# Weight tiles split as whole tiles instead of as two halves, in a two-block network on one core

## The chip, the cores and the metric

The kernel runs on one core of one Trainium2 chip, as one launch. The metric is device time in microseconds (us) of that launch. The profile is of one profiled execution of the same kernel.

## The reference, cut to what matters

512 tokens of width 1024 (and 256 context tokens) pass through two blocks. The first block is a mixer (a gated linear scan in both directions and a chunk-wise spatial gating), then a mixture of experts: 64 experts of width 256, of which each token uses 8, and one shared expert. The second block is a mixer of windowed attention and chunk-wise retention, then an MLP with a squared ReLU. All products are float32. The part that the change touches most:

```python
def swiglu(h, w_gu, w_down):
    gate, up = jnp.split(h @ w_gu, 2, axis=-1)
    return (jax.nn.silu(gate) * up) @ w_down

def moe_ffn(h, w_router, b_router, w_gu, w_down, w_sh_gu, w_sh_down):
    ...
    def expert_block(acc, blk):
        tok, wts, e = blk
        out = swiglu(h_pad[tok], w_gu[e], w_down[e])
        return acc.at[tok].add(out * wts[:, None].astype(out.dtype)), None
    ...
    return acc[:N] + swiglu(h, w_sh_gu, w_sh_down)
```

The other large products are of the same kind (`h @ w_in`, `y @ w_o`, `merged @ w_out`, `hdn @ w_ff2`): activations for 512 tokens against a weight matrix that is read once.

## The kernel before, in words

**A product as three.** A float32 product is made of three products of reduced values. Each operand is cut into a high part (`hi`, the value rounded by a copy) and a low part (`lo`, the value less its high part), and `mm3` (L142 to L148) issues hi x hi (L146), hi x lo (L147) and lo x hi (L148) into one accumulator. Where the weights are the second operand, as in the experts, L147 reads the low part of the weights and L148 the low part of the activations, when the names in the rows read `mm<-whi,eaT` in either order: the rows name the buffers of both operands, whichever is loaded as weights.

**A unit.** Weights come in units of 2048 values a partition, 1 MB each. `load_unit` (L113) gives a unit a raw buffer (`raw`, three of them, and two more from the pool `wraw2` in the expert layer) and issues one DMA on SP's queue. `split_unit` (L121) cuts it: `hi` is an ACT copy (L132, `whi` in the rows), `lo` a subtraction on DVE (L133, `wlo`; a few are given to POOL). A unit of 2048 values is cut in two pieces of 1024 values, each with its own `hi` and `lo` buffer, its own ACT copy and its own subtraction; the class `Rows` (L55) finds the piece in which row k of the unit lies. A unit of 1024 values (`w_branch_a`, `w_branch_b`, `w_att_up`) is one piece.

**The rings.** The buffers for pieces are the pool `wsplit`, six for `hi` and six for `lo`, taken in turn by `Turns` (L42): three units. In the expert layer `grow` (L1130) adds the pool `wsplit2` with two more, so four units. `each_unit` (L1372), which serves the four quarters of a matrix that are all in use at once, adds two of the pool `wsplit3`, taken after the first two units. A buffer is free for its next piece when the last matmul that reads it is done.

**The expert layer** (`experts`, L1170). `plan` (L1149) puts the tokens of the experts into 44 groups with 47 blocks of up to 128 rows; 64 experts have three units each, two of `w_expert_gu` and one of `w_expert_down`, 192 in all. A unit serves twelve matmuls of 512 columns for each block of its expert. For each group the program says, in this order: the first gu unit; then, by `advance`, the turning of the *previous* group's activations (`expert_turn`, L1014: two transposes `tp` on PE, then `split_ps`, L150, whose high part `eaT` is an ACT copy, L152, and whose low part `eaT` is a DVE subtraction, L153); the second gu unit; then the previous group's down unit with `eaT` as the other operand (`expert_out`, L1025), whose result is scaled by ACT into `ey`. Behind that, `expert_parts` (L1043) cuts part of the rows into `eys` (high part on ACT, L1048, low part on POOL, L1049) for a one-hot product into accumulators (`expert_add`, L1054), and the rest goes out by scattering DMAs of POOL (L1039). Tables of slots (`slot_tables`, L892 to L940: one-hots `oh` on DVE, L903, their matmuls, L908, and small sums) and gathers of rows on POOL (L981) come ahead of the groups that need them.

**Order.** Outside two stretches that are ordered by hand (ACT in the linear scan, and DVE, ACT and POOL where the two blocks meet), a planner orders each engine's instructions ahead of the run: it goes by expected durations and by the program's order as priority, and an engine then runs its instructions in that fixed order, each as its waits allow. So an instruction that is ready on the chip can stand behind one that is not, or behind a long one.

The change touches `PIECES`, `PIECE` and `Rows` (L30, L55), the pool `wsplit` in the constructor, `split_unit`, `fm_chunk` (L162, which reads the number of rows of a unit), `grow` and the line that restores the rings behind it (L1146), and `each_unit`.

Of the kernel before, what the change touches and what calls it, by code (L numbers as in the profile page):

```python
# [10 lines left out]
F = mybir.dt.float32  # L11
R = mybir.dt.float32r
# [3 lines left out]
AF = mybir.ActivationFunctionType  # L16
# [10 lines left out]
KD = D // 128  # L27
EPS = 1e-6
UNIT = 2048
PIECES = 2  # L30
PIECE = UNIT // PIECES


VEC = {}
# [7 lines left out]
class Turns:  # L42


    def __init__(self, *pools):
        self.pools = list(pools)
        self.n = 0

    def next(self):
        order = [p for p, n in self.pools for _ in range(n)]  # L50
        self.n += 1
        return order[(self.n - 1) % len(order)]


class Rows:  # L55


    def __init__(self, tiles, n, a):
        self.tiles, self.n, self.rows = tiles, n, a

    def __getitem__(self, at):
        p, k, *rest = at
        return self.tiles[k // self.n][(p, k % self.n, *rest)]


class Kernel:
    def __init__(self, ctx, tc, ins, out):
        self.tc, self.nc, self.ins, self.out = tc, tc.nc, ins, out
        self.ctx = ctx
        pool = lambda name, bufs=1, **k: ctx.enter_context(tc.tile_pool(name=name, bufs=bufs, **k))  # L70
        self.const = pool("const")
        self.raws = Turns((pool("wraw", RAW_BUFS, side="right"), RAW_BUFS))
        self.splits = Turns((pool("wsplit", SPLIT_BUFS * PIECES), SPLIT_BUFS * PIECES))
        self.dram = pool("scratch", space=DRAM)
        self.background, self.ticking = iter(()), False
        self.constants()
# [44 lines left out]
    def split_unit(self, parts, a, b, engine=None, rv=None):  # L121

        nc = self.nc
        if rv is None:
            rv = self.load_unit(parts if isinstance(parts, list) else [(None, parts)], a, b)
        n = min(a, a * PIECE // UNIT) if a * b == UNIT else a
        tiles = []
        for k in range(0, a, n):
            sp = self.splits.next()
            hi = sp.tile([128, PIECE], R, tag="hi", name="whi")[:, :n * b].rearrange("p (a b) -> p a b", a=n)  # L130
            lo = sp.tile([128, PIECE], R, tag="lo", name="wlo")[:, :n * b].rearrange("p (a b) -> p a b", a=n)
            nc.scalar.activation(hi, rv[:, k:k + n], AF.Copy)  # L132
            (engine or nc.vector).tensor_sub(lo, rv[:, k:k + n], hi.bitcast(F))  # L133
            tiles.append((hi, lo))
        hv, lv = (Rows([t[i] for t in tiles], n, a) for i in range(2))
        if not self.ticking:
            self.ticking = True
            next(self.background, None)
            self.ticking = False
        return hv, lv  # L140

    def mm3(self, ps, a, b, start, stop):  # L142

# [17 lines left out]

    def fm_chunk(self, ps, w, x, j, n=T, x0=0):  # L162

        kk = w[0].rows
        for k in range(kk):
            self.mm3(ps, [y[:, k, j * 128:(j + 1) * 128] for y in w],
                     [y[:, k, x0:x0 + n] for y in x], k == 0, k == kk - 1)
# [919 lines left out]
    def first_block(self):  # L1087

        nc, tc, ins = self.nc, self.tc, self.ins
        dram = lambda name, n, m=D: self.dram.tile([n, m], F, name=name)  # L1090
        h2d, x1d, cb = dram("h2d", T), dram("x1d", T), dram("cb", T, D - CA)
        self.g3d = dram("g3d", 1)
        rctx, hctx = ExitStack(), ExitStack()
        yT, rows = self.mixer(rctx)
        actx = ExitStack()
        pp = actx.enter_context(tc.tile_pool(name="moeps", bufs=1, space=PSUM))
        with tc.tile_pool(name="route", bufs=1) as keep:
            self.routing_state(keep)
            hp = hctx.enter_context(tc.tile_pool(name="h2T", bufs=1))

            h2T = [[hp.tile([128, KD, T // 2], R, name=f"h2T{h}{i}") for i in range(2)] for h in range(2)]
            pt = tc.tile_pool(name="b1o", bufs=1, space=PSUM)
            ap = tc.tile_pool(name="moeacc", bufs=1, space=PSUM)
            raws, splits = self.raws, self.splits
            with ExitStack() as mctx, ExitStack() as ectx:
                with pt as pt:
                    out = self.out_proj(pp, pt, yT, rows, h2T, h2d, x1d)
                    next(out)
                    rctx.close()
                    mp = mctx.enter_context(tc.tile_pool(name="moe", bufs=1, side="right"))  # L1110
                    acc, gp = [], []
                    gT = [mp.tile([128, 2, T], R, name=f"shT{i}") for i in range(2)]
                    shared = self.shared_expert(mp, pp, gp, gT, h2T)
                    for _ in range(SHARED_EARLY):
                        next(shared)
                    for _ in out:
                        pass
                gctx = ExitStack()
                gp.append(gctx.enter_context(tc.tile_pool(name="moegu", bufs=1, space=PSUM)))

                def sums():

                    gctx.close()
                    ap_ = actx.enter_context(ap)
                    acc.extend(ap_.tile([128, 512], F, name=f"acc{t}") for t in range(NT))

                rawp = ectx.enter_context(tc.tile_pool(name="wraw2", bufs=RAW2, side="right"))
                self.raws = Turns(*raws.pools, (rawp, RAW2))

                def grow():  # L1130
                    hctx.close()
                    sp = ectx.enter_context(tc.tile_pool(name="wsplit2", bufs=PIECES))
                    self.splits = Turns(*splits.pools, (sp, PIECES))
                    return ectx.enter_context(tc.tile_pool(name="moe2", bufs=1))

                def ahead():

                    more = self.raws
                    self.raws = Turns(*raws.pools)
                    self.first_raws = self.quarters("w_v_2")[:RAW_BUFS]  # L1140
                    self.first_raws = [self.load_unit([(None, w)], 4, 512) for w in self.first_raws]
                    self.raws = Turns(more.pools[1])
                    self.splits = Turns(self.splits.pools[1])

                more = self.experts(mp, pp, h2d, cb, acc, shared, gT, sums, grow, ahead, ectx)
            self.raws, self.splits = raws, splits  # L1146
        return x1d, cb, acc, more, actx.close

    def plan(self):  # L1149
# [221 lines left out]

    def each_unit(self, ctx, w, loaded=(), engines=()):  # L1372

        sp = ctx.enter_context(self.tc.tile_pool(name="wsplit3", bufs=PIECES))
        (base, n), = self.splits.pools
        loaded = [*loaded, *[None] * 4]
        engines = [*engines, *[None] * 4]
        splits = self.splits
        turns = Turns((base, n - PIECES), (sp, PIECES), (base, PIECES))
        for q, rv, e in zip(w, loaded, engines):  # L1380
            self.splits = turns
            unit = self.split_unit(q, 4, 512, e, rv)
            self.splits = splits
            yield unit
# [428 lines left out]
SPLIT_BUFS = 3  # L1813
# [146 lines left out]
```

## Time and profile before

| | |
|---|---|
| runs | 2130.84, 2125.3, 2128.33 us; median 2128.33 |
| profiled execution | 2128.15 us, span 2126.4 us, mean granted clock 0.985 |
| PE matmul, busy | 2038.1 us (96%), 10311 instructions |
| PE weight load, busy | 1663.4 us (78%) |
| DVE, busy | 1425.5 us (67%) |
| ACT, busy | 1090.8 us (51%) |
| POOL, busy | 486.2 us (23%) |
| `wlo` on DVE (L133) | 586 instructions, 728.0 us |
| `whi` on ACT (L132) | 592 instructions, 621.0 us |
| DMA | 386.68 MB, mean 182 GB/s |

The span is the time from the first to the last instruction of the profiled execution; the execution's own time holds the little that lies around it. PE is the engine of the matmuls and PEld its weight loads, which run beside them; DVE, ACT and POOL are the vector, scalar and GpSimd engines; SP issues DMAs. Matmuls overlap in their pipeline, so that PE's busy share says that it has work, not how fast that goes. An idle time is put down to the instruction whose end released the engine. L followed by a number is a line of the kernel; `split_unit` and `mm3` are helpers, so that all weights share their lines, and the names of the tiles tell products apart (`xT`, `eaT` in the expert layer; `hT`, `x`, `mg` and others elsewhere).

### The profile page before, as it was taken

The page shows a single profiled execution, that of the slowest core. Times are in us where ns is not written, and L with a number is a line of the kernel's source. Part 1 is how long each engine was busy: PE and PEld are TensorE (multiplying, and loading weights), DVE is VectorE, ACT ScalarE, POOL GpSimd, SP SyncE. Part 2 cuts the span into 40 slices and gives each one's busy share as a digit, 9 for nine tenths or more (in the row PEclk, how much of TensorE's full clock was granted, in tenths as well). Part 3 has the DMA queues.
Part 4 walks back from the last instruction along what each step waited for, and adds up shares of the span by engine and source line. Part 5 has one row for each costly group of instructions (what it writes and reads, how often), then busy time and mean ns, then how long its engine had stood idle before and what let it go on. Part 6 is the DMA issues. An engine that isn't in the chain of part 4 may idle for free. (4 is left out here: it accounts for less than half of the span.)

```text
span 2126.4 us, 28083 instructions
## 1 busy us (share of the span) xinstructions
PE 2038.1 (96%) x10311; PEld 1663.4 (78%) x10311; DVE 1425.5 (67%) x2444; ACT 1090.8 (51%) x1569; POOL 486.2 (23%) x307
## 2 busy tenths in 40 slices
PE   7999999999899999999999996999999999999998
PEld 4777888877787788877887784877788878888886
DVE  6667767647899799989999785455853345333344
ACT  7445443233387788878887884334232224232232
POOL 0322231011144343524334213011100001010110
PEclk9999999999899999999999998999999999999999
DMA  7211136633499899999999885312122333222221
GB/s 297 70 41 48 53 111 261 235 110 147 177 322 335 290 341 352 339 325 307 337 336 337 289 290 188 132 60 70 50 89 79 114 115 116 92 100 99 99 80 40
DMA packets 69713, 386.68 MB, mean 182 GB/s; under 512 B 11374, under 2 KB 12351, under 8 KB 30020
## 3 DMA queue, kind: packets, MB, share of 16 engines
q1 hardware_dynamic: 56932, 357.56, 45.6%
q0 software_dynamic: 12640, 27.29, 5.5%
q8 instruction: 82, 1.34, 0.2%
q14 instruction: 59, 0.48, 0.1%
HBM read 369.99 MB, written 23.55 MB: 185 GB/s over the span
## 5 line engine op out<-in xcount | busy, mean ns | idle before, releaser
L133 DVE TENSOR_TENSOR wlo<-raw,whi 128x1024 fp32r<-128x1024 f32 x586 | 728.0, 1258 | 252.0 <-ACT whi L132 244.0
L132 ACT ACTIVATE whi<-raw 128x1024 fp32r<-128x1024 f32 x592 | 621.0, 1057 | 385.6 <-PE mm L147 190.7
L146 PE MATMUL mm<-whi,xT 128*128 128x512 f32 (+2 forms) x536 | 219.7, 410 | 0.1
L147 PE MATMUL mm<-wlo,xT 128*128 128x512 f32 (+2 forms) x536 | 211.9, 395 | 0.0
L148 PE MATMUL mm<-whi,xT 128*128 128x512 f32 (+2 forms) x536 | 211.9, 395 | 0.0
L1039 POOL DMA_INDIRECT cb<-ey,sgi x67 | 130.9, 1954 | 233.4 <-ACT ey L1035 148.4
L146 PE MATMUL mm<-hT,whi 128*128 128x512 f32 x320 | 127.0, 397 | 0.0
L147 PE MATMUL mm<-hT,whi 128*128 128x512 f32 x320 | 125.8, 394 | 0.0
L148 PE MATMUL mm<-hT,wlo 128*128 128x512 f32 x320 | 125.5, 392 | 0.0
L147 PE MATMUL mm<-x,whi 128*128 128x512 f32 x304 | 122.5, 403 | 0.0
L148 PE MATMUL mm<-x,wlo 128*128 128x512 f32 x304 | 120.8, 398 | 0.0
L146 PE MATMUL mm<-x,whi 128*128 128x512 f32 x304 | 120.8, 397 | 0.0
L148 PEld LDWEIGHTS mm<-whi,xT 128*128 128x128 f32 (+2 forms) x536 | 96.8, 181 | 27.8
L146 PEld LDWEIGHTS mm<-whi,xT 128*128 128x128 f32 (+2 forms) x536 | 97.2, 181 | 23.1 <-DVE act L1012 0.5
L1565 POOL TENSOR_TENSOR relu<-relu 128x512 f32<-128x512 f32 x32 | 42.9, 1341 | 315.0 <-ACT relu L1563 315.0
L147 PEld LDWEIGHTS mm<-wlo,xT 128*128 128x128 f32 (+2 forms) x536 | 97.2, 181 | 22.3
L1049 POOL TENSOR_TENSOR eys<-ey,eys 128x384 fp32r<-128x384 f32 (+2 forms) x47 | 79.2, 1686 | 141.2 <-ACT eys L1048 114.3
L148 PE MATMUL mm<-whi,eaT 128*128 128x512 f32 (+2 forms) x268 | 105.8, 396 | 0.4 <-DVE eaT L153 0.2
L147 PE MATMUL mm<-wlo,eaT 128*128 128x512 f32 (+2 forms) x268 | 105.8, 395 | 0.0
L146 PE MATMUL mm<-whi,eaT 128*128 128x512 f32 (+2 forms) x268 | 105.8, 395 | 0.0
L146 PE MATMUL mm<-y,whi 128*128 128x512 f32 (+2 forms) x272 | 103.2, 380 | 0.0
L148 PE MATMUL mm<-y,wlo 128*128 128x512 f32 (+2 forms) x272 | 103.1, 379 | 0.0
(534 smaller groups left out, 4488.9 us busy)
## 6 DMA issues: line engine op xcount, KB each, us to landing
raw<-in_w_expert_gu SPq DMA_DIRECT2D x128, 1024.0 KB
raw<-in_w_expert_down SPq DMA_DIRECT2D x64, 1024.0 KB
raw<-in_w_in SPq DMA_DIRECT2D x41, 1024.0 KB
raw<-in_w_ff SPq DMA_DIRECT2D x32, 1024.0 KB
raw<-in_w_ada SPq DMA_DIRECT2D x24, 1024.0 KB
raw<-in_w_out SPq DMA_DIRECT2D x8, 1024.0 KB
raw<-in_w_v SPq DMA_DIRECT2D x4, 1024.0 KB
raw<-in_w_ret_up SPq DMA_DIRECT2D x4, 1024.0 KB
```

The lines of the kernel that those rows point to most:

```text
L132: nc.scalar.activation(hi, rv[:, k:k + n], AF.Copy)
L133: (engine or nc.vector).tensor_sub(lo, rv[:, k:k + n], hi.bitcast(F))
L146: mm(ps, ah, bh, start=start, stop=False)
L147: mm(ps, ah, bl, start=False, stop=False)
L148: mm(ps, al, bh, start=False, stop=stop)
L1039: self.nc.gpsimd.indirect_dma_start(out=cb, out_offset=bass.IndirectOffsetOnAxis(ap=gi, axis=0), in_=y[p0:p1, CA:], in_offset=None, bounds ...
L1049: last = nc.gpsimd.tensor_sub(yl, y[0:m, :CA], yh.bitcast(F))
L1565: nc.gpsimd.tensor_mul(sq, r, r)
```

## The change

A unit has one `hi` and one `lo` buffer of 2048 values instead of two of each. The rings hold as many units as before: three in `wsplit`, one more in `wsplit2` and in `wsplit3`. `self.cuts` says in how many instructions each part of a unit is written: two of 1024 values as before, into halves of the one buffer, and one of 2048 values in the expert layer, from `grow` until the rings are restored. A unit of 1024 values takes a whole buffer and is written by one instruction, as before. The order of the matmuls in the program, the raw buffers and the loads stay.

```diff
-PIECES = 2
-PIECE = UNIT // PIECES
...
-class Rows:
...
-        self.splits = Turns((pool("wsplit", SPLIT_BUFS * PIECES), SPLIT_BUFS * PIECES))
+        self.splits = Turns((pool("wsplit", SPLIT_BUFS), SPLIT_BUFS))
+        self.cuts = 2
...
-        n = min(a, a * PIECE // UNIT) if a * b == UNIT else a
-        tiles = []
+        n = a // self.cuts if a * b == UNIT else a
+        sp = self.splits.next()
+        hi, lo = (sp.tile([128, UNIT], R, tag=t, name="w" + t)[:, :a * b].rearrange("p (a b) -> p a b", a=a)
+                  for t in ("hi", "lo"))
         for k in range(0, a, n):
-            sp = self.splits.next()
-            hi = sp.tile([128, PIECE], R, tag="hi", name="whi")[:, :n * b].rearrange("p (a b) -> p a b", a=n)
-            lo = sp.tile([128, PIECE], R, tag="lo", name="wlo")[:, :n * b].rearrange("p (a b) -> p a b", a=n)
-            nc.scalar.activation(hi, rv[:, k:k + n], AF.Copy)
-            (engine or nc.vector).tensor_sub(lo, rv[:, k:k + n], hi.bitcast(F))
-            tiles.append((hi, lo))
-        hv, lv = (Rows([t[i] for t in tiles], n, a) for i in range(2))
+            nc.scalar.activation(hi[:, k:k + n], rv[:, k:k + n], AF.Copy)
+            (engine or nc.vector).tensor_sub(lo[:, k:k + n], rv[:, k:k + n], hi[:, k:k + n].bitcast(F))
...
-        return hv, lv
+        return hi, lo
...
-        kk = w[0].rows
+        kk = w[0].shape[1]
...
-                    sp = ectx.enter_context(tc.tile_pool(name="wsplit2", bufs=PIECES))
-                    self.splits = Turns(*splits.pools, (sp, PIECES))
+                    sp = ectx.enter_context(tc.tile_pool(name="wsplit2", bufs=1))
+                    self.splits = Turns(*splits.pools, (sp, 1))
+                    self.cuts = 1
...
-            self.raws, self.splits = raws, splits
+            self.raws, self.splits, self.cuts = raws, splits, 2
...
-        sp = ctx.enter_context(self.tc.tile_pool(name="wsplit3", bufs=PIECES))
+        sp = ctx.enter_context(self.tc.tile_pool(name="wsplit3", bufs=1))
...
-        turns = Turns((base, n - PIECES), (sp, PIECES), (base, PIECES))
+        turns = Turns((base, n - 1), (sp, 1), (base, 1))
```

## Rows read from the trace of the kernel before

**Rows 1.** Windows: us, busy by engine, granted clock, DMA share, GB/s.
```profile
600.00:1272.00 672.00, 668.01 (x3415) 532.01 (x3414) 605.40 (x881) 557.26 (x742) 262.91 (x148) 1.00 0.92 323
1590.00:2067.00 477.00, 475.70 (x2140) 394.10 (x2139) 182.99 (x216) 148.73 (x184) 50.59 (x38) 1.00 0.29 102
```

**Rows 2.** Waits, 600 to 1272: total us, times, longest.
```profile
ACT whi L132 <- PE mm L148: 71.2, 136, 5.5
...
PEld L908 <- DVE oh L903: 4.6, 9, 1.2
...
PEld acc L1058 <- POOL eys L1049: 2.2, 3, 1.2
...
PEld mm L148 <- DVE eaT L153: 1.9, 4, 0.7
```

**Rows 3.** Lines by form, 600 to 1272: busy us, mean ns, idle before and its releasers.
```profile
L133 DVE TENSOR_TENSOR wlo<-raw,whi 128x1024 fp32r<-128x1024 f32 x372 | 458.2, 1253 | 54.8 <-ACT whi L132 50.6
L132 ACT ACTIVATE whi<-raw 128x1024 fp32r<-128x1024 f32 x371 | 390.0, 1057 | 74.2 <-PE mm L148 71.2 <-DVE wlo L133 0.7 <-DVE srow L915 0.3
...
L1048 ACT ACTIVATE eys<-ey 128x384 fp32r<-128x384 f32 x30 | 15.7, 524 | 0.8
```

**Rows 4.** Tiles wlo and hdl: ns shortest/median/longest, first and last start.
```profile
L133 DVE TENSOR_TENSOR wlo<-raw,whi x586: 1201/1221/2776, 22.3 to 2075.7; 128x1024 fp32r<-128x1024 f32 x196
L153 DVE TENSOR_TENSOR hdl<-relu,hdh x32: 691/693/694, 1780.8 to 2078.5; 128x512 fp32r<-128x512 f32 x32
```

**Rows 5.** Timeline of ACT: start, us, instruction, [idle before, releaser].
```profile
857.66 1.06 ACT L132 ACTIVATE whi<-raw 128x1024 fp32r<-128x1024 f32 x1 [0.45 <-PE mm L148]
...
865.31 1.06 ACT L132 ACTIVATE whi<-raw 128x1024 fp32r<-128x1024 f32 x1 [0.18 <-PE mm L148]
866.28 0.37 ACT L152 ACTIVATE eaT<-tp 128x256 fp32r<-128x256 f32 x1
```

**Rows 6.** Timeline of DVE, same stretch.
```profile
858.70 4.62 DVE L133 TENSOR_TENSOR wlo<-raw,whi 128x1024 fp32r<-128x1024 f32 x4
...
866.00 2.35 DVE L133 TENSOR_TENSOR wlo<-raw,whi 128x1024 fp32r<-128x1024 f32 x2
868.27 0.42 DVE L153 TENSOR_TENSOR eaT<-tp,eaT 128x256 fp32r<-128x256 f32 x1
```

**Rows 7.** Timeline of PE and its weight loads, same stretch.
```profile
865.25 0.48 PE L146 MATMUL mm<-whi,xT 128*128 128x512 f32 x1
...
868.13 0.39 PE L146 MATMUL mm<-whi,eaT 128*128 128x512 f32 x1
868.37 0.40 PE L147 MATMUL mm<-wlo,eaT 128*128 128x512 f32 x1
...
868.74 0.19 PEld L148 LDWEIGHTS mm<-whi,eaT 128*128 128x128 f32 x1 [0.41 <-DVE eaT L153]
```

**Rows 8.** Timeline of DVE in a later group.
```profile
1016.96 0.36 DVE L153 TENSOR_TENSOR eaT<-tp,eaT 128x192 fp32r<-128x192 f32 x1
1017.24 2.35 DVE L133 TENSOR_TENSOR wlo<-raw,whi 128x1024 fp32r<-128x1024 f32 x2
```

**Rows 9.** Timeline of PE in the retention stage.
```profile
1506.44 0.60 PE L1773 MATMUL ryps<-rv,ram 128*128 128x256 f32 x2
1507.77 0.48 PE L147 MATMUL mm<-x,whi 128*128 128x512 f32 x1
```

**Rows 10.** Timeline of PE ahead of the second block's output product.
```profile
1724.03 0.50 PE L147 MATMUL mm<-wlo,mg 128*128 128x512 f32 x1 [0.54 <-DVE wlo L133]
```

**Rows 11.** Timeline of DVE and POOL in the expert layer.
```profile
855.72 2.66 DVE L133 TENSOR_TENSOR wlo<-raw,whi 128x1024 fp32r<-128x1024 f32 x1 [0.22 <-ACT whi L132]
...
856.25 1.03 POOL L1049 TENSOR_TENSOR eys<-ey,eys 96x384 fp32r<-96x384 f32 x1
```

**Rows 12.** Tile hT: ns shortest/median/longest, first and last start.
```profile
L146 PE MATMUL mm<-hT,whi x320: 387/389/501, 43.5 to 463.5; 128*128 128x512 f32 x160
...
L153 DVE TENSOR_TENSOR hT<-hm,hT x8: 671/685/693, 26.4 to 55.9; 128x512 fp32r<-128x512 f32 x8
```

More of the change, by code (lines that the diff above doesn't have):

```diff
@@ L52, in next @@
         return order[(self.n - 1) % len(order)]
-class Rows:
[L58 to L63, printed above, removed]
 class Kernel:
```

## The prediction, made before the kernel was run

> **What bounds the kernel now.** I read the windows first, because the shares of the whole span average stages with different limits. In the expert layer, here 600 to 1272 us, the reader is to see four resources near their limit at once [rows 1]: PE is busy 668.01 of 672 us, DVE 605.40 (90%), ACT 557.26 (83%), and the DMA share is 0.92. In the stretch of the MLP, 1590 to 2067 us, PE is as full (475.70 of 477) while DVE has 38% and ACT 31%. So a change that lightens DVE and ACT can matter in the expert layer alone, and there only if they hold PE up.
>
> Do they? The waits say no. ACT's own splits wait for matmuls, 71.2 us in 136 waits [rows 2]: the consumer is the slow one, and the split runs into full buffers. PE's weight loads wait little: 4.6 us for the one-hot of the tables, 2.2 for POOL's eys, 1.9 for the low part of eaT [rows 2]; no wait for whi or wlo is among PE's longest. The timeline shows the lead: the whi that starts at 857.66 [rows 5] and its wlo, done at the latest when four of them end at 858.70 + 4.62 = 863.32 [rows 6], feed the matmul at 868.13 [rows 7]. The buffers hold four units, so a unit is split up to four ahead of its use, here at least 868.13 - 863.32 = 4.8 us before it. PE bounds the expert layer; elsewhere it does so too, but for the stalls between stages.
>
> **The change, part by part.** The base is the profiled execution, 2128.15 us, of which the span is 2126.4; the median of three runs is 2128.33, so the sum serves for both.
>
> 1. Shorter work. An expert's unit of 2048 values has two ACT copies of 1.057 us and two DVE subtractions of 1.253 in the mean [rows 3], 1.221 in the median [rows 4]. No row has 2048 values, so I extend the line: ACT takes 0.524 us for 384 values and 1.057 for 1024 [rows 3], 0.83 ns a value, so about 1.057 + 0.85 = 1.91 (estimate); DVE takes 0.693 for 512 and 1.221 for 1024 [rows 4], so about 1.221 + 1.06 = 2.28 (estimate). Saved per unit: 2.11 - 1.91 = 0.20 us of ACT and 2.44 - 2.28 = 0.16 of DVE, over 64 experts x 3 units 39 and 31 us. All of it lies beside PE: 0 on the path. What it can give back is some of PE's waits for DVE, 4.6 + 1.9 [rows 2]: I take 3 us off.
>
> 2. Later release. A whole buffer is free when the last of its twelve matmuls is done, not half of it at the middle. The ring holds four units as before, so the first value of a new split comes up to half a unit later, about 1.4 us (six matmuls, 868.13 - 865.25 being one unit's twelve and 2.88 us [rows 7]). With the merged pair, wlo is complete some 1.4 + 1.91 + 2.28 - 3.6 = 2.0 us later (3.6 is about what 1.06 and two of 1.22 take now). The lead of at least 4.8 us covers it: 0. The raw buffer also returns later, and SP, which issues its loads in order, starts the next ones later by as much; ACT's waits name PE [rows 2], not a DMA, so five raw buffers cover that: 0. Without these covers it would be up to 2 us on each of 192 units.
>
> 3. What queues behind a long instruction. This is the step that costs. Between the two gu units of a group the previous group's activations are turned: PE tp, ACT eaT (high), DVE eaT (low), and three matmuls into the next unit PE needs the low part. Read one group [rows 5 to 7]: at 865.31 ACT takes a whi released by PE, so eaT starts at 866.28, right behind it; DVE takes two wlo from 866.00 (2.35 us) and eaT only at 868.27; PE's load waits 0.41 us, till 868.74. With whole units the same order reads: whi 865.31 to 867.22, eaT high to about 867.5, still ahead of its matmul at 868.13. But wlo is ready at 867.25, before eaT, and runs to 869.55; eaT low ends about 869.95, and the matmul that would start at 868.60 (one spacing after the 868.37 of [rows 7]) is 1.4 us late. Nothing can go between the halves any more. If DVE instead takes eaT first, as it does at 1016.96 before the wlo pair of 1017.24 [rows 8], it ends by 867.95 and PE loses nothing. Which comes first is set by the planner's order, and DVE in that order may still be busy until eaT is ready. Bounds over 44 groups: 0 to 44 x 1.4 = 62 us. The planner also fills PE's waits where it foresees them: in the retention stage it puts ryps matmuls between those of a gate product [rows 9]. Today only 4 loads are late for eaT [rows 2], so I take the value nearer the lower end, one group in five: 9 x 1.4 = 13 us.
>
> 4. Outside the expert layer the instructions stay; only release is coarser, and a unit of 1024 values takes a whole buffer. A product there lasts 48 matmuls, some 11 us, and three buffers leave two products of lead: 0. Where four units are wanted at once, before out_proj's tiles of the second block, PE already waits 0.54 us for a wlo at 1724.03 [rows 10]; one more wlo of 1.2 us now comes after the last release. I add 1 us, bounds 0 and 3 for the three such places.
>
> 5. GpSimd. While POOL subtracts eys for 1.03 us from 856.25, the DVE wlo of 855.72 takes 2.66 [rows 11] instead of 1.22: one of the two blocks the other. An instruction of 2.28 can hold eys up by 1.06 more. PE waits for eys 3 times now, 2.2 us [rows 2]; I take 0, bound 47 x 1.06 = 50 us of POOL time, of which PE sees at most a few.
> The Trainium skill (SBUF — State Buffer, section "SBUF: two separate sides") has a rule against the change here: DVE with two SBUF inputs and a GpSimd op share a port pair, and whichever starts first keeps it for its whole instruction while the other fully blocks. The trace agrees that they exclude each other, but in these rows DVE started first and was the one drawn out; by the rule the sum would hold up to 1.06 us more for each eys met.
>
> Sum: 2128.15 - 3 + 13 + 1 = 2139.
>
> **The rivals.**
> *Slower by waits for eaT (the forecast).* 2135 to 2190, by one to six of seven groups late; for it the order in rows 5 to 7, against it the planner's freedom.
> *No change.* Every delay stays under its lead, or PE's waits are filled: 2128 - 3 + 1 = 2126 to 2134. For it PE's 668 of 672 us; against it that eaT has no lead of four units.
> *Faster, DVE the true limit.* If DVE at 90% of the layer set the pace, its 31 us would come off: 2128 - 31 = 2097; if only half of PE's waits of some 9 us [rows 2] and a few hidden ones went, about 2120. Against it ACT waits for PE, not PE for wlo; the point from which it decides is a wlo that ends after its matmul could start. The Trainium skill (Perfetto Trace Analysis, "Identifying the Most-Contended Engine") calls matmul busy time a bad measure and would judge by weight-load busy time. That is 532 of 672, 79% [rows 1], under DVE's 90%, so by the page DVE is the most contended and 2097 the result. In the timeline matmuls follow each other at 0.24 us with no wait named [rows 7], which speaks for PE.
> *The change does not do what it says.* If one buffer made a matmul wait for both parts, the stages with two parts would start later by 1.2 us a unit wherever there is no lead, some 10 us in all. Against it: matmuls on hT begin at 43.5 us while its parts are written until 55.9 [rows 12], so a wait is for the part read.
>
> **How the numbers follow.** A measurement of this kernel can tell about 0.3% from no change, 6.4 us. Slower by waits: 0.42, and with the last rival's 0.02 the slower side has 0.44. No change 0.37. Faster 0.19, of which the full 2097 has 0.04. The prediction is the likeliest case, 2139, with its own range 2135 to 2190. For 8 in 10 I go down to 2117, which leaves out the full gain, and up to 2172, where 31 of 44 groups would be late.
>
> **What would show it.** In the expert layer's rows: 192 whi at 1.91 and 192 wlo at 2.28 us; ACT's waits on PE longer, its splits starting at unit ends; DVE and ACT busy less by some 30 and 38 us; PE loads of L148 waiting for DVE eaT, some 9 or more times at up to 1.4 us, against 4 now. PE full and those waits unchanged would make it the second case; a wait of PE for wlo would show that a lead I called safe was not; gaps in PE that DVE or POOL used to cause gone, and the time near 2120, the third. A stage outside the expert layer longer by over 3 us would make part 4 wrong.

## The result, and the profile after

The changed kernel takes 2142.33 us in the median (2141.41 to 2148.84, 4 runs) against 2127.07 before (2125.30 to 2130.84, 4 runs): the ratio is 1.0078, with a 95% interval of 1.0056 to 1.0099. It is slower, by 15 us in the medians. The profiled execution took 2141.41 us with a span of 2139.7, so 13.3 us more than the span before; the account below is made against that.

Lines have moved: `whi` is now L119 and `wlo` L120, the three products of `mm3` L131 to L133, the two parts of `eaT` L137 and L138, `oh` L888, `eys` L1034 and the one-hot product `acc` L1043. Each experiment below has its own numbers; the tile names tell.

**Where it went.** First the place. These are rows of the tile `eaT` between 590 and 1310 us, for the last product of each kernel (ns shortest/median/longest, first and last start). Before:

```profile
L148 PE MATMUL mm<-whi,eaT x268: 387/394/506, 599.6 to 1282.5; 128*128 128x512 f32 x102, 128*96 128x512 f32 x26, 128*64 128x512 f32 x6
```

After:

```profile
L133 PE MATMUL mm<-whi,eaT x268: 387/394/505, 599.0 to 1295.9; 128*128 128x512 f32 x102, 128*96 128x512 f32 x26, 128*64 128x512 f32 x6
```

The last matmul on `eaT` starts 13.4 us later, and the first 0.6 us earlier. As the span grew by 13.3 us, the whole loss lies in the expert layer; all that comes behind it takes as long as it did.

The window of the expert layer after, with the columns of [rows 1]:

```profile
600.00:1272.00 672.00, 661.08 (x3355) 524.96 (x3355) 571.92 (x687) 514.07 (x546) 283.89 (x146) 0.99 0.91 320
```

Against [rows 1] DVE has 33.5 us less work in the same 672 us and ACT 43.2 less. PE got through 3355 matmuls instead of 3415, so part of the difference is work not yet reached: the window holds 182 whole subtractions where it held 372 halves, 186 units, and four units are some 10 us of DVE. Lighter helpers, and a slower kernel: the load that was taken off was not what PE waited for. The lines by form in the same window:

```profile
L120 DVE TENSOR_TENSOR wlo<-raw,whi 128x2048 fp32r<-128x2048 f32 x182 | 420.2, 2318 | 83.1 <-ACT whi L119 81.9
L119 ACT ACTIVATE whi<-raw 128x2048 fp32r<-128x2048 f32 x181 | 346.1, 1912 | 66.6 <-PE mm L133 66.1
```

A whole copy takes 1.912 us and a whole subtraction 2.318 in the mean, against two of 1.057 and two of 1.253 [rows 3]. The instructions did what the change meant them to do. The waits in the same window:

```profile
ACT whi L119 <- PE mm L133: 66.1, 56, 8.6
...
PEld mm L133 <- DVE eaT L138: 4.8, 14, 1.0
PEld mm L131 <- DVE eaT L138: 4.1, 2, 2.1
...
PEld L893 <- DVE oh L888: 1.4, 4, 0.5
```

PE's loads now wait 8.9 us for DVE's `eaT`, 16 times, against 1.9 us and 4 times [rows 2] (and 0.2 us once on L146, which those rows leave out). The wait for `oh` went down, from 4.6 to 1.4 us. ACT's splits wait for PE 56 times where they did 136 times, in all about as long: a whole buffer comes free half as often.

**What such a wait looks like.** One group, in the timelines of ACT, DVE and PE (start, us, instruction, idle before and its releaser). ACT:

```profile
685.72 1.92 ACT L119 ACTIVATE whi<-raw 128x2048 fp32r<-128x2048 f32 x1 [8.63 <-PE mm L133]
687.54 0.31 ACT L137 ACTIVATE eaT<-tp 128x192 fp32r<-128x192 f32 x1
```

DVE:

```profile
687.66 2.29 DVE L120 TENSOR_TENSOR wlo<-raw,whi 128x2048 fp32r<-128x2048 f32 x1 [2.70 <-ACT whi L119]
689.88 0.35 DVE L138 TENSOR_TENSOR eaT<-tp,eaT 128x192 fp32r<-128x192 f32 x1
```

PE:

```profile
685.98 0.33 PE L1005 MATMUL tp<-ident,act 96*128 96x96 f32 x2
...
688.26 0.40 PE L133 MATMUL mm<-whi,xT 128*128 128x512 f32 x1
690.28 0.48 PE L131 MATMUL mm<-whi,eaT 128*96 128x512 f32 x1 [1.62 <-DVE eaT L138]
```

ACT had been idle for 8.63 us and DVE for 2.70. A unit's last matmul frees a whole buffer, ACT takes the whole copy, and the two transposes come 0.26 us behind its start. From there all is in line: copy, `eaT` high, whole subtraction, `eaT` low, and PE stands for 1.62 us. No engine was short of time; a long instruction began just ahead of a short one that PE needed. One thing is open here: the matmul that starts at 690.28 is the product hi x hi, which does not read the low part. The trace gives the end of the low part, at 690.23, as its releaser and does not say what of that instruction it needed. Two of the five stops for `eaT` are of this kind; the other three are of L133, which reads the low part.

Mostly the planner saw this coming and put other matmuls in between. In the group of [rows 5 to 7] PE's row after is:

```profile
872.94 1.23 PE L1043 MATMUL acc<-eys,eoh 96*128 96x384 f32 x6
874.00 0.49 PE L133 MATMUL mm<-whi,eaT 128*128 128x512 f32 x1
```

Six one-hot matmuls now stand between the first products on `eaT` and those that read its low part, which DVE delivers from 873.52 to 873.94. Counted over the timelines, DVE's `eaT` comes directly behind a whole subtraction in 31 of the 47 turnings, and directly behind a half in 31 of 47 before. PE stands for it five times.

### The profile page after: what moved, and what is told of

Read it like the earlier page. It is cut to its first block, busy times and chain, and to the rows that moved or that the text cites. A ratio compares the mean times of both kernels' runs of the same rounds, so it can differ in the third digit from the quotient of the medians.

```text
span 2139.7 us, 27507 instructions
## 1 busy us (share of the span) xinstructions
PE 2042.2 (95%) x10311; PEld 1664.4 (78%) x10311; DVE 1412.4 (66%) x2251; ACT 1050.7 (49%) x1376; POOL 514.0 (24%) x307
## 5 line engine op out<-in xcount | busy, mean ns | idle before, releaser
L120 DVE TENSOR_TENSOR wlo<-raw,whi 128x1024 fp32r<-128x1024 f32 (+1 forms) x393 | 708.4, 1818 | 290.6 <-ACT whi L119 285.1
L119 ACT ACTIVATE whi<-raw 128x1024 fp32r<-128x1024 f32 (+1 forms) x399 | 579.8, 1468 | 400.3 <-PE mm L132 211.2
L131 PE MATMUL mm<-whi,xT 128*128 128x512 f32 (+2 forms) x536 | 220.2, 411 | 0.9 <-DVE act L997 0.9
L133 PE MATMUL mm<-whi,xT 128*128 128x512 f32 (+2 forms) x536 | 214.1, 399 | 0.0
L1024 POOL DMA_INDIRECT cb<-ey,sgi x67 | 137.8, 2056 | 231.4 <-ACT ey L1020 129.6
L131 PE MATMUL mm<-hT,whi 128*128 128x512 f32 x320 | 126.9, 397 | 0.0
L133 PE MATMUL mm<-hT,wlo 128*128 128x512 f32 x320 | 125.5, 392 | 0.0
L131 PE MATMUL mm<-x,whi 128*128 128x512 f32 x304 | 121.2, 399 | 0.0
L133 PE MATMUL mm<-x,wlo 128*128 128x512 f32 x304 | 120.1, 395 | 0.0
L133 PEld LDWEIGHTS mm<-whi,xT 128*128 128x128 f32 (+2 forms) x536 | 97.6, 182 | 27.4
L131 PEld LDWEIGHTS mm<-whi,xT 128*128 128x128 f32 (+2 forms) x536 | 97.8, 182 | 24.3 <-DVE act L997 1.3
L966 POOL DMA_INDIRECT xg<-h2d,sgi x47 | 95.1, 2023 | 81.6 <-issue 25.8
L131 PE MATMUL mm<-whi,eaT 128*128 128x512 f32 (+2 forms) x268 | 106.1, 396 | 5.2 <-DVE eaT L138 3.2
L1034 POOL TENSOR_TENSOR eys<-ey,eys 128x384 fp32r<-128x384 f32 (+2 forms) x47 | 75.5, 1606 | 135.2 <-ACT eys L1033 123.6
L1020 ACT ACTIVATE ey<-mm,swt 64x512 f32<-64x512 f32 (+3 forms) x134 | 89.0, 679 | 36.4 <-issue 23.4
L133 PE MATMUL mm<-whi,eaT 128*128 128x512 f32 (+2 forms) x268 | 102.6, 402 | 1.6 <-DVE eaT L138 1.2
```

The costliest lines, as they stand in the source:

```text
L119: nc.scalar.activation(hi[:, k:k + n], rv[:, k:k + n], AF.Copy)
L120: (engine or nc.vector).tensor_sub(lo[:, k:k + n], rv[:, k:k + n], hi[:, k:k + n].bitcast(F))
L131: mm(ps, ah, bh, start=start, stop=False)
L133: mm(ps, al, bh, start=False, stop=stop)
L966: self.nc.gpsimd.indirect_dma_start(out=xg[0:gi.shape[0]], out_offset=None, in_=h2d, in_offset=bass.IndirectOffsetOnAxis(ap=gi, axis=0), b ...
L1020: nc.scalar.activation(y[p0:p1, sl], ps[p0:p1], AF.Copy, scale=wt[p0:p1])
```

## The experiments

Theory A: a whole instruction stands in front of a short one that PE waits for. Rival B: whole buffers come free later, so the splits run late. All times are medians beside the kernel before on the same chip; edits are to the changed kernel. A fifth buffer in the ring would test B from the other side; no run here has one, and there is no number 10. The waits shown are of one execution of each kernel; in experiments 2, 4 and 5 it took some 4 us more than the median, in 1 it took 2 us less.

**1. Whole buffers, halves as instructions.**

```diff
-                    self.cuts = 1
+                    self.cuts = 2
```

> The changed kernel with two copies and two subtractions of 1024 values in the expert layer too; the buffers stay whole. Theory A (a 2048-value instruction stands in front of the eaT chain): the coarser release costs nothing, so about the time of the kernel before, 2126 to 2132 us, with PE waits for DVE eaT in the expert layer back near 2 us. Rival B (whole buffers come free later and the splits run late): 2138 to 2145, as the changed kernel.

2128.82 us against 2127.81, ratio 1.0006 (0.9995 to 1.0018). The waits in the expert layer, 600 to 1285 us:

```profile
PEld acc L1043 <- POOL eys L1034: 2.5, 3, 1.5
...
PEld mm L133 <- DVE eaT L138: 0.7, 2, 0.5
```

The loss is gone, and with it B as a cause by itself: with whole buffers everywhere and halves as instructions nothing changes. The loss needs the longer instructions, and the order that the planner makes with them.

**2 and 3. One engine's instruction whole.** In both the loop over pieces is written as two, of `na` rows for ACT and `nd` for DVE, in the expert layer.

```diff
+        na, nd = (n, a // 2) if self.cuts == 1 else (n, n)      # 2: the copy is whole
+        na, nd = (a // 2, n) if self.cuts == 1 else (n, n)      # 3: the subtraction is whole
```

> The changed kernel with one ACT copy of 2048 values and two DVE subtractions of 1024 in the expert layer. A: the high part of eaT is still late by the longer copy, the low part can go between the halves or behind one of them: 2129 to 2137. B: as the changed kernel, 2138 to 2145.

> The changed kernel with two ACT copies of 1024 values and one DVE subtraction of 2048 in the expert layer. A: most of the cost lies in the low part of eaT behind the whole subtraction, so 2133 to 2142, more than with the whole copy alone. B: 2138 to 2145.

With the copy whole: 2135.43 against 2127.81, 1.0035 (1.0021 to 1.0049). With the subtraction whole: 2140.79, 1.0069 (1.0052 to 1.0085). Waits of PE's loads, copy whole:

```profile
PEld mm L135 <- DVE eaT L140: 8.6, 21, 0.9
PEld L895 <- DVE oh L890: 4.5, 9, 0.8
```

Subtraction whole:

```profile
PEld L895 <- DVE oh L890: 6.9, 9, 1.0
...
PEld mm L133 <- DVE eaT L140: 3.8, 2, 2.1
```

Either does harm, the longer instruction more, as A had it; together (1.0078) they cost hardly more than the subtraction alone. But A spoke of `eaT`, and with the subtraction whole the loads wait longest for `oh`, another short product of DVE (6.9 us, against 5.8 for `eaT` on L133 and L135); PE itself stands 3.1 us for `oh` and 3.3 for `eaT`. And a late load is not yet a stop of PE: with the copy whole the loads wait 10.6 us for DVE's `eaT` on the two lines, more than in the changed kernel, while PE stands 1.6 us for it, and none of its stops over 0.15 us names the high part, of which the expectation spoke.

**4. `eaT` first.** The splits of the fourth to the eleventh unit behind a turning are put behind the turning's two `eaT` instructions, each on its own engine; the fourth is the one that takes the buffer freed just before the turning.

```diff
+        with ExitStack() as behind:
...
+                for at, act, dve in self.turns[-4:]:
+                    if at <= self.unit_no - 4 and at > self.unit_no - 12:
+                        behind.enter_context(self.tc.issue_after(act))
+                        behind.enter_context(self.tc.issue_after(dve))
```

> The changed kernel, whole instructions kept; the splits of the units from four further on are put behind the eaT copy on ACT and the eaT subtraction on DVE, so that eaT goes first. A: the loss goes, 2122 to 2131. B, where instruction order was not the cause: 2138 to 2145, or longer, as the splits start later.

2150.95 against 2127.81, 1.0104 (1.0084 to 1.0123). A missed here. The waits of the expert layer, ACT's ahead of those of PE's loads:

```profile
ACT eaT L144 <- PE tp L1012: 81.3, 39, 11.0
...
PEld L900 <- DVE oh L895: 6.3, 9, 1.4
...
PEld tp L1012 <- DVE act L1004: 5.0, 1, 5.0
...
PEld mm L140 <- DVE eaT L145: 1.3, 3, 0.6
```

The wait for `eaT` fell from 8.9 to 1.3 us, as wanted. But ACT now stands for 81.3 us in front of `eaT` until the transposes are done, and the splits that come late meet other short instructions instead: PE itself stands 7.1 us for `act`, 7.0 for `xT` and 2.6 for `oh`.

**7. `eaT` first on DVE alone** (the same edit with the line for `act` left out, and only for the unit four further on).

> The changed kernel, whole instructions; on DVE alone the subtraction of the unit four behind a turning is put behind the low part of eaT; ACT's order stays free. If in the fourth run the loss came from ACT standing idle for tp: 2127 to 2136 here. If it came from DVE, where what is put behind eaT comes in the way of xT, oh and act instead: 2138 to 2150.

2143.15 against 2128.38, 1.0074 (1.0060 to 1.0088). The waits of PE and its loads:

```profile
PEld L899 <- DVE oh L894: 5.6, 9, 1.6
...
PE tp L899 <- DVE xT L144: 5.0, 3, 1.9
...
PEld mm L137 <- DVE act L1003: 3.1, 3, 1.2
...
PEld mm L139 <- DVE eaT L144: 1.5, 3, 0.7
```

The wait for `eaT` is small again and the loss is the whole loss. ACT's idle time was not the reason alone. The timelines show what took the place of `eaT`: nearly all of PE's stops in the layer, 9.6 of 10.5 us, are for an instruction of DVE that came behind a whole subtraction, directly or with one to three short ones between, and 5.5 us of them are for `xT`, 0.2 for `eaT`. A whole instruction has to stand somewhere, and here most places on DVE had a short instruction behind them that PE wanted.

**5 and 6. Cut where it meets the turning, or whole only there.**

```diff
+            near = self.unit_no - 4 in self.turns or self.unit_no - 3 in self.turns
+            n = a // 2 if near else a      # 5
+            n = a if near else a // 2      # 6
```

> The changed kernel with whole instructions in the expert layer, but the units three and four behind each turning of the activations (those whose split meets eaT on ACT and DVE) cut in two: about 83 units of two, the other half whole. Theory A, narrowed after the first four runs (only the long instruction that meets eaT costs): 2125 to 2133 us, waits of PE for eaT near 2 us. Rival C (any short instruction of ACT or DVE that PE waits for, xT, oh and act as well, is held up by any whole one): half of the loss stays, 2132 to 2139.

> The reverse: only the units three and four behind each turning are written by whole instructions, the others in two. A: nearly all of the loss, 2136 to 2144. C: half of it, 2131 to 2137.

Cut there: 2133.49 against 2128.38, 1.0021 (1.0012 to 1.0031). Whole only there: 2139.38, 1.0050 (1.0037 to 1.0064). The waits of PE's loads, cut at the turning:

```profile
PEld L897 <- DVE oh L892: 4.9, 8, 1.2
PEld mm L137 <- DVE eaT L142: 4.3, 5, 1.5
```

Whole at the turning:

```profile
PEld mm L137 <- DVE eaT L142: 7.5, 21, 1.0
...
PEld mm L135 <- DVE eaT L142: 4.1, 2, 2.1
```

The two losses, 5.1 and 11.0 us, add up to 16.1; that of the changed kernel is 15.3, and 13.7 on the chip of these two (8). Some two thirds go with the whole units that meet the turning (A), a third with the others. The first time lies just outside A's range and inside C's, the second inside A's: neither theory has it alone. And the third is not shown to be rival C's: in the trace of 5, of the 7.5 us that PE stands for DVE, 1.8 are for instructions behind a whole subtraction and 5.7 for instructions behind a half, two of which were drawn out to nearly 3 us.

**9 and 11. Shorter still.** Whole buffers, halves on ACT, and on DVE four subtractions of 512 values, for the units near a turning (9) or for all of the layer (11).

```diff
+            flat = [x[:, k:k + n].rearrange("p a b -> p (a b)") for x in (lo, rv, hi)]
+            for c in range(0, n * b, q):      # q = 512 where wanted, else 1024
+                l, r, h = (x[:, c:c + q] for x in flat)
+                (engine or nc.vector).tensor_sub(l, r, h.bitcast(F))
```

> Whole buffers, halves as in the first run, but the units three and four behind each turning get four DVE subtractions of 512 values instead of two of 1024: 88 units, by 4 x 0.69 - 2 x 1.22 = 0.33 us each 29 us more of DVE work. If the length of what stands in front of a short instruction is all that counts: 2123 to 2129 us. If DVE's amount of work in the layer counts (rival L): 2130 to 2140.

> The same with four subtractions of 512 values for every unit of the expert layer: some 63 us more of DVE work, so about 668 of the 672 us of the window. Length alone: 2123 to 2132. L: DVE has no slack left and becomes the bound, 2140 to 2190.

Near a turning: 2133.36 against 2128.67, 1.0020 (1.0007 to 1.0033). All: 2144.13, 1.0069 (1.0054 to 1.0085). In 9 more than half of PE's stops in the layer, 4.3 of 7.5 us, are one:

```profile
PE acc L1050 <- POOL eys L1041: 4.3, 1, 4.3
```

The window of the expert layer in 11:

```profile
600.00:1272.00 672.00, 660.36 (x3359) 526.16 (x3358) 620.40 (x1241) 529.87 (x729) 296.40 (x145) 0.99 0.91 321
```

and its waits of PE and its loads:

```profile
PE acc L1048 <- POOL eys L1039: 4.1, 3, 2.3
...
PE mm L135 <- DVE act L1001: 3.4, 1, 3.4
...
PE tp L897 <- DVE oh L892: 2.2, 4, 1.4
...
PEld mm L136 <- DVE wlo L124: 1.9, 3, 0.8
...
PEld mm L137 <- DVE eaT L142: 1.1, 2, 0.5
```

The wait for `eaT` is nearly gone, as the length of the pieces has it, and yet the kernel is as slow as with whole instructions. Both times lie in rival L's range, at its mild end, but L's cause is not shown: DVE was to be full with 668 us and has 620, against 605 before. A few waits name `wlo`, which is in none of the lists above (PE itself stands 0.7 us for it); most of the stops name POOL's `eys`, one `act` and `oh`. The stop of 3.4 us for `act` stands at the end of a chain that began with ACT waiting 5.36 us for a scattering DMA. In the trace of 9 the growth is one late `eys` and a fall of the clock behind it (table in the next section). What the shorter pieces have to do with either stays open. With the copies in halves, subtractions of 512, 1024 and 2048 values cost +0.69% (11), nothing (1) and +0.69% (3).

**8. The changed kernel again**, for a second profile.

> The changed kernel again, unaltered, for a second profile: 2139 to 2146 by every theory. If the falls of PE's granted clock inside the expert layer follow from the stalls, they come at the same places, behind the stalls near 678 and 1153 us; if they are chance, elsewhere or not at all.

2142.04 us (2 runs) against 2128.38, 1.0064 (1.0045 to 1.0082). The waits of the loads for `eaT` are the same to 0.1 us. Of the clock, the section on what was not expected.

## Why the prediction was right, and where not

The time (2139 forecast, 2142.33 measured) and the side were right, and the reason named for it, `eaT` late behind a whole subtraction, is the largest single cause of the stops that appeared. That the number came so near is in part luck, as the third point shows. Point by point:

- **Shorter work.** The two estimates held: 1.91 us forecast and 1.912 measured, 2.28 and 2.318. The gain was put at 3 us of PE's waits. The wait of the loads for `oh` did shrink by 3.2 us, but PE itself had stood only 1.2 us for `oh`, which is all that came back, and the same lighter DVE served `eaT` worse.
- **Later release: 0.** Shown by experiment 1, with halves. With whole instructions the release at a unit's end is also the moment at which the long copy starts, next to the transposes, so release and length work together; with short instructions the same release does no harm.
- **What queues behind a long instruction: 13 us.** Right in kind; the size was wrong, and other members made up the sum. I counted the waits of loads, but loads run beside matmuls: in [rows 7] the load was 0.41 us late and the matmul 0.14 behind its spacing. What counts is PE's own idle time, over the layer to its end. Before (window, with the columns of [rows 1], and a wait):

```profile
600.00:1285.00 685.00, 680.20 (x3470) 541.70 (x3469) 613.24 (x889) 567.55 (x755) 269.21 (x152) 1.00 0.92 323
```
```profile
PE mm L148 <- DVE eaT L153: 0.2, 1, 0.2
```

  After:

```profile
600.00:1298.00 698.00, 685.28 (x3462) 543.32 (x3461) 593.28 (x702) 535.59 (x570) 291.13 (x152) 0.99 0.90 317
```
```profile
PE mm L131 <- DVE eaT L138: 3.2, 2, 1.6
...
PE mm L131 <- DVE xT L138: 1.5, 1, 1.5
...
PE tp L893 <- DVE xT L138: 1.3, 1, 1.3
PE mm L133 <- DVE eaT L138: 1.2, 3, 0.6
```

  PE is idle for 12.7 us instead of 4.8, and up to 5.3 us more come from a granted clock that I did not have in the sum (below): 13.2 of the 13.4 us. Of the stops, `eaT` has 4.4 us in five, where I had nine groups of 1.4, 13 us. The rest of the growth is 2.1 us more for `xT`, 0.9 for `act`, 1.5 for `eys` and 0.5 for the high part of `eaT`, less 1.2 for `oh`. Every stop for DVE, 8.1 us in all, is for an instruction that came directly behind a whole subtraction. Nor was it one group in five that stood behind one, but 31 turnings of 47; the planner covered most of them, as the bound from below foresaw. So the term that I put at 13 us came to 4, and 13 is right only with other short instructions and the clock.

  The same count for every run, of the stretch from the first to the last start of a matmul on `eaT`. "Clock lost" adds, over stretches of 25 us with a granted clock under 1.00, the shortfall times 25:

| kernel | stretch, us | PE idle, us | clock lost, us |
|---|---|---|---|
| before | 683.4 | 4.7 | 0 |
| 1, halves | 681.5 | 3.4 | 0 |
| changed | 698.1 | 12.7 | 5.3 |
| 8, changed again | 695.1 | 11.4 | 3.5 |
| 2, copy whole | 691.7 | 7.3 | 3.5 |
| 3, subtraction whole | 693.6 | 12.9 | 0 |
| 4, `eaT` first | 711.1 | 19.8 | 12.3 |
| 7, first on DVE | 696.1 | 11.0 | 7.0 |
| 5, cut at turning | 691.1 | 10.9 | 0 |
| 6, whole at turning | 694.3 | 12.6 | 1.8 |
| 9, 512 near turning | 688.8 | 7.7 | 5.0 |
| 11, 512 | 697.0 | 12.5 | 5.3 |

  In every run idle time and clock together give the growth of the stretch to within 3 us. The price of the long instructions is paid in both.
- **The step that failed** is the sentence that DVE need only take `eaT` first and "PE loses nothing". In experiments 4 and 7 it does take it first (`eaT` comes directly behind a `wlo` in 4 and 8 of 47 turnings), the waits of the loads for `eaT` fall to 1.3 and 1.5 us, and the kernel takes 2150.95 and 2143.15 us. I had looked at one short instruction; DVE has several kinds (`eaT`, `xT`, `act`, `oh`) on which PE depends, and the long one only changes its victim.
- **Outside the layer: 1 us, bounds 0 and 3.** The end of the layer moved by 13.4 us and the span by 13.3, so about 0; experiment 1, which has the coarser buffers everywhere, says the same. At the place of [rows 10] PE now waits 0.68 us, for a `whi` at 1736.99, instead of 0.54.
- **GpSimd: 0.** Waits of PE's loads for `eys` went from 2.2 to 2.9 us, PE's own stops for both parts of it from 2.1 to 3.6; the 50 us of bound stayed far off. The pair of [rows 11] is not the usual one: of 23 pairs in the trace before in which DVE's `wlo` began first and POOL's `eys` ran into it, `wlo` kept its 1.21 to 1.23 us in 21, and in 20 of these `eys` took longer than the 1.0 to 1.1 us that it mostly takes alone: 1.15 us and more.
- **The rivals.** "No change" is outside the interval. "Faster, DVE the true limit" fell by its own test: over the whole layer DVE has 20.0 us less work (613.24 and 593.28 above) and PE waits for DVE more. By the rule of the Trainium skill (Perfetto Trace Analysis, "Identifying the Most-Contended Engine") DVE, busier than PE's loads, was the compute engine to lighten first; I left out the page's measure for the DMA. The trace shows the contrary for this step. "Both parts waited for" did not occur: experiment 1 has one buffer with parts written one by one, at the time of before.

Why a third of the loss is left when the units at the turning are cut (experiment 5) stays open: its stops are for `oh`, `xT`, `act`, `eaT` and `eys`, mostly behind halves. Before and in experiment 1, where all are halves, PE's stops behind them come to 2.2 and 1.1 us.

## What to carry to other kernels

On an engine with a fixed order, merging instructions saves their fixed cost and can make everything short behind them wait for up to their length: look not at the busy share, but at the small instructions of that engine whose results the bounding engine needs within a few microseconds, and compare their slack with the length of what would stand before them. Moving one of them ahead was no cure here, where there are several. Of the three lengths tried 1024 values was best, with 0.7% lost at half and at double; why at half stays open. And buffers can be merged without merging the instructions that fill them.

## What the runs showed that was not expected

A stall of PE can cost twice. Before, the granted clock is 1.00 throughout the layer's window [rows 1]. After, two stretches of 25 us have less (columns of [rows 1]):

```profile
675.00:700.00 25.00, 21.30 (x120) 16.46 (x118) 18.43 (x35) 13.26 (x16) 8.66 (x7) 0.93 0.88 280
...
1150.00:1175.00 25.00, 22.72 (x119) 17.70 (x118) 16.40 (x31) 15.29 (x16) 9.33 (x7) 0.86 0.78 269
```

0.07 x 25 and 0.14 x 25 are 1.8 and 3.5 us of full clock, 5.3 together, less where PE waited anyway. In the timeline of PE, ahead of the first:

```profile
677.28 1.49 PE L1043 MATMUL acc<-eys,eoh 128*128 128x384 f32 x7 [0.81 <-POOL eys L1034]
680.03 0.50 PE L893 MATMUL tp<-raux,oh 128*96 128x6 bf16 x12 [1.27 <-DVE xT L138]
...
683.25 0.63 PE L133 MATMUL mm<-whi,xT 128*128 128x512 f32 x1
683.68 0.63 PE L131 MATMUL mm<-whi,xT 128*128 128x512 f32 x1
```

PE had stood for 0.81 and 1.27 us within 3 us; behind that matmuls follow at 0.43 us, the 1.2 GHz level, against 0.24 in [rows 7], where the clock is 1.00, the 2.4 GHz level; from 684.8 on they follow at 0.23 to 0.24 again. In the second profile of the same kernel (experiment 8) the fall near 680 to 690 is there again, and the other is not at 1150 but earlier:

```profile
675.00:700.00 25.00, 21.32 (x120) 16.36 (x119) 19.98 (x37) 13.34 (x17) 11.03 (x7) 0.93 0.90 307
925.00:950.00 25.00, 22.94 (x120) 17.52 (x119) 20.55 (x34) 16.48 (x19) 7.32 (x6) 0.93 0.86 323
1150.00:1175.00 25.00, 22.67 (x132) 17.81 (x131) 19.08 (x33) 17.05 (x19) 10.09 (x7) 1.00 0.82 305
```

So the falls go with stalls, but a stall does not always bring one. And they are not the whole loss: here 0.07 x 25 twice, 3.5 us in all, in a kernel that is as slow, and in experiment 3, which loses 13 us, PE is idle as long as in the changed kernel and no stretch of 25 us in the layer shows less than 1.00.
